# New durations and a shape-change term in the clock that orders a hybrid encoder kernel

## Chip, cores and metric

The kernel runs on one core of a Trainium2 chip. The metric is the time of one execution in microseconds of device time; the time before is the median of three runs.

## What is computed

One layer of a streaming encoder, for 512 prompt tokens and 8 x 16 sample tokens (640 rows, 1024 wide, all float32). Two mixers read one projection of the normalised input; their outputs are gated, merged and projected.

```python
h = rmsnorm(x); proj = h @ w_in                # q,k,v,z_A | g_A,g_B | r,k,v,lora_w,lora_a,z_B
# A: stick-breaking attention, 16 heads x 64, s < t only
z = q @ k.T / 8
later = reverse_cumsum(log_sigmoid(-z)) - log_sigmoid(-z)
o_a = exp(log_sigmoid(z) + later) @ v
# B: RWKV-7 recurrence, 16 heads, state S of 64 x 64
S = S * w_t + (S @ -kk_t) (kk_t * a_t) + v_t k_t ;  o_b = S @ r_t
y = sig(g_A) * ((o_a * silu(z_A)) @ w_o_a) + sig(g_B) * ((norm(o_b) * silu(z_B)) @ w_o_b)
out = rmsnorm(x + y @ w_out)
```

## The kernel before, in words

The kernel is one static program: a Python function emits every instruction in order, and each engine works through its own queue in that order, held only by semaphores.

Projections are jobs of 128 output columns (`gemm_range`): two halves of 320 or 322 tokens, 8 depth tiles, and three matmuls for each (weights and activations are split into a high and a low part, `whi`, `wlo` and `xh`, `xl`, in the fp32r type), all into the PSUM tile `ps_g`. They are the filler: after every 6 matmuls the generator yields. The split of the next job's weights (`wsplit` on ScalarE, `wlow` on VectorE) stands at fixed places in the job.

Everything else is a stream, a generator that yields the tiles its next step reads. For each of 8 head pairs of mixer B: `prep` (decay, keys, the tiles `H`, `BK`, `AB`), `prep2` (a triangular solve, 30 steps of two products on POOL in `INV` and `itmp`, then transposes through `STG`), `samp`, `chain` (8 recurrence steps of three PE parts: `X,H` into `RH`, `RH,AB` into `X`, `X,BKt` into the next `X`), `sstate` and `post`. For each of 8 head pairs of mixer A: `aprep` (loads, transposes) and `attn`, nine score items, each two sigmoids on ScalarE (`kp`, `bt`), a mask product on POOL, a reversed scan and a product on VectorE, four or fewer transposes by PE two items later (`flip`, into `wt`), and the product with the values (`pv`) one item after that.

What goes next is decided while the program is built, by `Driver.run` and `Clock`. Every engine call goes through `_Eng`, which computes a duration `d` by engine and operation and hands it to `Clock.note`; this keeps when each engine is free and when each tile is ready (end plus a hop `LAT` of 0.25 us, of which `near` is taken off on the same engine). The driver takes PE's clock as now. A stream whose tiles are ready by then steps at once, lowest priority number first; when none is, the projections emit 6 more matmuls. `SLACK` (3 us) holds the solver near PE, `CALM` (1.6 us) holds `prep` when VectorE's clock runs ahead, `MARGIN` (3 us) delays stores on SP's queue. All of these are in units of this clock. The clock is used only to build the order; it is no instruction.

The last six projection blocks (`w_o_a`, `w_out`) run after the streams, in a fixed order.

Of the kernel before, what the change touches and what calls it, by code (L numbers as in the profile page):

```python
# [26 lines left out]
F32 = mybir.dt.float32  # L27
F32R = mybir.dt.float32r
# [53 lines left out]
class Clock:  # L82
# [5 lines left out]
    def __init__(self):  # L88
        self.free = dict(pe=0.0, act=0.0, dve=0.0, pool=0.0, dma=0.0)
        self.ready = {}  # L90
        self.by = {}
        self.used = {}
        self.rings = {}
        self.closed = 0.0
        self.tbl = None
        self.last = {}
        self.near = dict(pe=0.25, act=0.2, dve=0.2, pool=0.15, dma=0.0)
        self.wire = 0.0

    def bank(self, tag, bufs, name):  # L100
# [46 lines left out]
def _name(ap):  # L147

    if not hasattr(ap, "tensor"):
        return ap  # L150
    n = ap.tensor.name
    return f"{n}:{ap.offset % (8 * T) // T}" if n in PARTS else n


def _cols(ap):
    n = 1
    for d in ap.shape[1:]:
        n *= d
    return n
# [30 lines left out]
class _Eng:  # L190
# [3 lines left out]
    def __getattr__(self, op):  # L194
        f = getattr(self.obj, op)

        def call(*a, **k):
            r = f(*a, **k)  # L198
            aps = [x for x in list(a) + list(k.values()) if hasattr(x, "tensor")]
            out = k.get("out", aps[0])  # L200
            ins = [x for x in aps if x is not out]
            n = _cols(out)
            e = self.eng
            lat = Clock.LAT
            if e == "pe":
                w = k.get("lhsT")
                if w is None:
                    d = 0.115
                else:
                    m = _cols(w)  # L210
                    if w.dtype == F32R:
                        d = max(n / 2360.0, 0.107)
                    elif w.dtype == F32:
                        d = max(0.026 + n * 0.00087, 0.082 if m > 32 else 0.041) if m <= 64 else 0.005 + n / 600.0
                    else:
                        d = 0.06
            elif e == "act":
                d = 0.05 + n * 0.00086 + 0.1 * sum(hasattr(k.get(x), "tensor") for x in ("scale", "bias"))
                fn = str(k.get("func"))
                t = "sig" if "Sigmoid" in fn or "Tanh" in fn else "exp" if "Exp" in fn else \  # L220
                    "sqrt" if "Sqrt" in fn else None
                if t is not None and t != self.clk.tbl:
                    self.clk.tbl = t
                    d += 1.28
            elif e == "dve":
                d = 0.066 + n * 0.00105
                if "scalar" in op:
                    d += 0.03 * sum(hasattr(x, "tensor") and _cols(x) == 1 for x in list(a) + list(k.values()))
                if op == "reciprocal":
                    d = 0.05 + n * 0.0064  # L230
            elif e == "pool":
                d = 0.15 + n * (0.0021 if op == "tensor_tensor" else 0.001)
                if op == "tensor_copy":
                    d = 0.2 + n * 0.0035
            else:
                d = 0.47
                run = 2.0 if min(x.shape[-1] for x in aps) < 128 else 1.0
                lat = (n * out.shape[0] * 4 * run / 3.6e5, 0.65, 0.93)
            self.clk.note(e, d, [_name(x) for x in ins], [_name(out)], lat)
            return r  # L240
        return call
# [1455 lines left out]
```

## Time and profile before

| what | value |
|---|---|
| median of three runs | 1240.88 us (1238.41 to 1241.9) |
| profiled execution | 1238.89 us, span 1237.1 us |
| PE busy, of the span | 1181.2 us, 95% |
| VectorE, ScalarE, POOL busy | 757.6, 616.6, 601.5 us |
| granted TensorE clock, mean | 0.979 |

All times of the trace are us from the span's start. The span is four stages: a start to 41 us; projections with mixer B's streams, the recurrence stage, to 745 and with its last streams to 835; projections with mixer A's streams, the attention stage, to 1085; then projections alone. A busy PE is one with some matmul under way; matmuls overlap, and a projection matmul lasts 0.31 us while the next starts 0.15 us after it. A granted clock of 1.00 is 2.4 GHz, 0.50 is 1.2 GHz; other values are means over both. One float32 matmul of the program with few columns can stand as two in the trace.

### The profile page before, as it was taken

What the parts mean: (1) busy time and instruction counts of PE and PEld (TensorE: products, weight loads), DVE (VectorE), ACT (ScalarE), POOL (GpSimd) and SP (SyncE); (2) the same over time, 40 slices, a digit from 0 to 9 for tenths busy, and PEclk for the clock granted to TensorE, in tenths of its full rate; (3) what the DMA queues carried; (4) which work ended last, traced back from release to release, by engine and by line L of the source; (5) the groups of instructions that cost most, each with busy time, mean ns of one, the idle gap of its engine ahead of it and who ended that gap; (6) DMA issues with size and microseconds to landing.
All of it is one profiled execution on the core that took longest, in us unless ns stands there. A gap on an engine that the chain in (4) does not pass through costs nothing.

```text
span 1237.1 us, 24609 instructions
## 1 busy us (share of the span) xinstructions
PE 1181.2 (95%) x9538; PEld 1033.0 (84%) x9538; DVE 757.6 (61%) x1460; ACT 616.6 (50%) x1307; POOL 601.5 (49%) x867
## 2 busy tenths in 40 slices
PE   7999989999999999999999999999999989999997
PEld 5989977888878988878888797897777757899997
DVE  5475674965765767857658443337667787655334
ACT  5624446555556664574565563535555444513223
POOL 1032947728539659477395671034444473313302
PEclk8989999999999999999999999999999988999999
DMA  6232312222313313223133243388665577255322
GB/s 183 73 105 60 95 51 51 85 88 50 113 46 89 91 41 89 79 63 95 46 80 106 55 125 92 97 214 214 159 151 137 140 190 175 61 182 186 95 86 86
DMA packets 205292, 130.65 MB, mean 106 GB/s; under 512 B 78332, under 2 KB 184696, under 8 KB 205176
## 3 DMA queue, kind: packets, MB, share of 16 engines
q1 hardware_dynamic: 204888, 129.03, 37.3%
q8 instruction: 75, 1.23, 0.4%
q14 instruction: 41, 0.34, 0.1%
q0 software_dynamic: 288, 0.05, 0.0%
HBM read 97.70 MB, written 31.35 MB: 104 GB/s over the span
## 4 chain that ended last, share of the span: by engine, by line
PE 70%; DVE 13%; POOL 6%; ACT 6%; issue 3%; DMA 2%; SPq 0%; DVEq 0%; ACTq 0%; POOLq 0%
PE ps_g L198 47%; PE ps_a L198 10%; PE ps_b L198 8%; PE ps_c L198 4%; DVE kp L198 2%; POOL itmp L198 2%; DVE bt L198 1%; POOL INV L198 1%; ACT STG L198 1%; DVE wlo L198 1%; DMA raw<-in_w_o_a_dram 1%; ACT AB L198 1%; DVE xl L198 1%; DVE BK L198 1%; DVE Oa L198 1%
## 5 line engine op out<-in xcount | busy, mean ns | idle before, releaser
L198 PE MATMUL ps_g<-xh,whi 128*128 128x320 f32 (+1 forms) x1424 | 479.0, 336 | 1.3 <-ACT xh L198 1.3
L198 PE MATMUL ps_g<-xl,whi 128*128 128x320 f32 (+1 forms) x1424 | 445.4, 313 | 4.1 <-DVE xl L198 4.1
L198 PE MATMUL ps_g<-xh,wlo 128*128 128x320 f32 (+1 forms) x1424 | 445.4, 313 | 4.0 <-DVE wlo L198 4.0
L198 PEld LDWEIGHTS ps_g<-xh,whi 128*128 128x128 f32 x1424 | 271.5, 191 | 25.6 <-issue 10.4
L198 PEld LDWEIGHTS ps_g<-xl,whi 128*128 128x128 f32 x1424 | 272.0, 191 | 6.1 <-DVE xl L198 5.3
L198 PEld LDWEIGHTS ps_g<-xh,wlo 128*128 128x128 f32 x1424 | 271.4, 191 | 4.8 <-DVE wlo L198 4.8
L198 POOL TENSOR_TENSOR itmp<-INV 128x30 f32<-128x30 f32 (+14 forms) x240 | 138.3, 576 | 80.0 <-DVE INV L198 64.9
L198 POOL TENSOR_TENSOR INV<-INV,itmp 128x30 f32<-128x30 f32 (+14 forms) x240 | 146.2, 609 | 18.8
L198 DVE TENSOR_TENSOR wlo<-raw,whi 128x1024 fp32r<-128x1024 f32 x97 | 126.0, 1299 | 42.6 <-ACT whi L198 41.6
L198 ACT ACTIVATE whi<-raw 128x1024 fp32r<-128x1024 f32 x97 | 102.5, 1056 | 61.0 <-DMA raw<-in_w_o_a_dram 29.8
L198 POOL TENSOR_TENSOR bt<-bt,amsk 128x128 f32<-128x128 f32 x64 | 45.6, 716 | 130.6 <-ACT bt L198 62.0
L198 DVE TENSOR_TENSOR_SCAN kp<-kp,amsk 128x256 f32<-128x256 f32 (+3 forms) x80 | 75.8, 955 | 41.3 <-ACT kp L198 41.2
L198 ACT ACTIVATE sp<-ps_g 128x320 f32<-128x320 f32 x80 | 34.9, 437 | 84.6 <-PE ps_g L198 64.2
L198 ACT ACTIVATE kp<-ps_a 128x512 f32<-128x512 f32 (+3 forms) x72 | 33.1, 459 | 79.2 <-PE ps_a L198 61.9
L198 DVE SCALAR_TENSOR_TENSOR X<-ps_b,wc,SW 64x64 f32<-64x64 f32 x96 | 27.1, 283 | 73.4 <-PE ps_b L198 69.7
L198 POOL TENSOR_TENSOR ux<-X,cst 128x256 f32<-128x256 f32 x32 | 22.1, 713 | 98.2 <-DVE X L198 72.9
L198 ACT ACTIVATE RH<-ps_b 128x64 f32<-128x64 f32 (+1 forms) x64 | 15.1, 237 | 106.2 <-PE ps_b L198 106.0
L198 ACT ACT_TABLE_LOAD x39 | 50.0, 1283 | 10.6 <-DVE BK L198 6.0
L198 POOL TENSOR_TENSOR on<-on,V 128x640 f32<-128x640 f32 x8 | 13.0, 1621 | 86.6 <-ACT on L198 86.6
L198 DVE TENSOR_TENSOR bt<-bt,kp 128x511 f32<-128x511 f32 (+4 forms) x72 | 43.8, 608 | 9.4 <-POOL bt L198 2.9
L198 PE MATMUL ps_a<-H,BK 64*128 64x128 f32 x320 | 48.1, 286 | 0.7 <-DVE H L198 0.4
L198 PE MATMUL ps_b<-cst,bt 128*128 128x128 f32 x192 | 36.0, 294 | 12.9 <-DVE bt L198 12.4
(244 smaller groups left out, 2289.8 us busy)
## 6 DMA issues: line engine op xcount, KB each, us to landing
raw<-in_w_in_dram SPq DMA_DIRECT2D x81, 512.0 KB
q<-dr_q SPq DMA_DIRECT2D x32, 160.0 KB
Kr<-in_cache_sb_k_dram SPq DMA_DIRECT2D x16, 256.0 KB
Vp<-in_cache_sb_v_dram SPq DMA_DIRECT2D x16, 256.0 KB
raw<-in_w_o_b_dram SPq DMA_DIRECT2D x8, 512.0 KB
raw<-in_w_o_a_dram SPq DMA_DIRECT2D x8, 512.0 KB
oraw<-in_w_out_dram SPq DMA_DIRECT2D x4, 1024.0 KB
dr_zB<-zm SPq DMA_DIRECT2D x8, 320.0 KB
```

The lines of the kernel that those rows point to most:

```text
L198: r = f(*a, **k)
```

## The change

It replaces the constants by which `_Eng` computes a duration, and adds a term for PE: the shape of the part of the array that a matmul uses (rows above 32 or 64, columns above 32 or 64, with everything above 64 x 64 as "full") is kept in `Clock.mode`; a matmul of another shape than the one before is charged 0.1 us more when the array was in full use, 0.2 otherwise. On ScalarE it charges operations on fewer than 128 and fewer than 64 partitions more; on VectorE it has own formulas for scan, scalar-tensor-tensor, tensor-scalar, bn_stats and the strided transpose, and 0.09 more for reading PSUM on fewer than 128 partitions; POOL's constants rise. The two `near` values shrink. `LAT`, `SLACK`, `CALM`, `MARGIN`, the DMA constants and the driver's rules stay. No instruction is added, removed or resized: what can change is the order in which they are emitted, and with it each engine's queue.

```diff
--- before.py
+++ after.py
@@ -94,7 +94,8 @@
         self.closed = 0.0
         self.tbl = None
         self.last = {}
-        self.near = dict(pe=0.25, act=0.2, dve=0.2, pool=0.15, dma=0.0)
+        self.near = dict(pe=0.25, act=0.15, dve=0.14, pool=0.15, dma=0.0)
+        self.mode = None
         self.wire = 0.0
 
     def bank(self, tag, bufs, name):
@@ -204,18 +205,26 @@
             lat = Clock.LAT
             if e == "pe":
                 w = k.get("lhsT")
+                m, r = (128, 128) if w is None else (_cols(w), w.shape[0])
                 if w is None:
-                    d = 0.115
+                    d = 0.109
+                elif w.dtype == F32R:
+                    d = max(0.013 + n / 2400.0, 0.107)
+                elif w.dtype == F32:
+                    d = max(0.026 + n * 0.00087, 0.082 if m > 32 else 0.041) if m <= 64 else \
+                        max(n / 600.0 + 0.005, 0.216)
                 else:
-                    m = _cols(w)
-                    if w.dtype == F32R:
-                        d = max(n / 2360.0, 0.107)
-                    elif w.dtype == F32:
-                        d = max(0.026 + n * 0.00087, 0.082 if m > 32 else 0.041) if m <= 64 else 0.005 + n / 600.0
-                    else:
-                        d = 0.06
+                    d = 0.089
+                mode = "full" if r > 64 and m > 64 else (r > 32, r > 64, m > 32, m > 64)
+                if mode != self.clk.mode:
+                    d += 0.1 if self.clk.mode == "full" else 0.2
+                    self.clk.mode = mode
             elif e == "act":
-                d = 0.05 + n * 0.00086 + 0.1 * sum(hasattr(k.get(x), "tensor") for x in ("scale", "bias"))
+                d = 0.065 + n * 0.00085 + 0.1 * sum(hasattr(k.get(x), "tensor") for x in ("scale", "bias"))
+                if out.shape[0] < 64:
+                    d = 0.12 + n * 0.0021
+                elif out.shape[0] < 128:
+                    d += 0.115
                 fn = str(k.get("func"))
                 t = "sig" if "Sigmoid" in fn or "Tanh" in fn else "exp" if "Exp" in fn else \
                     "sqrt" if "Sqrt" in fn else None
@@ -223,15 +232,26 @@
                     self.clk.tbl = t
                     d += 1.28
             elif e == "dve":
-                d = 0.066 + n * 0.00105
-                if "scalar" in op:
-                    d += 0.03 * sum(hasattr(x, "tensor") and _cols(x) == 1 for x in list(a) + list(k.values()))
-                if op == "reciprocal":
+                d = 0.075 + n * 0.00106
+                if op == "scalar_tensor_tensor":
+                    d = 0.13 + n * 0.00112
+                elif op == "tensor_scalar":
+                    d = 0.1 + n * 0.0011 + 0.03 * sum(hasattr(x, "tensor") and _cols(x) == 1
+                                                     for x in list(a) + list(k.values()))
+                elif op == "tensor_tensor_scan":
+                    d = 0.03 + n * 0.0025
+                elif op == "reciprocal":
                     d = 0.05 + n * 0.0064
+                elif op == "bn_stats":
+                    d = 0.126
+                elif op == "transpose" and len(ins[0].shape) > 2 and ins[0].ap[-1][0] > 1:
+                    d = 2.03
+                if out.shape[0] < 128 and any(_name(x).startswith("ps_") for x in ins if hasattr(x, "tensor")):
+                    d += 0.09
             elif e == "pool":
-                d = 0.15 + n * (0.0021 if op == "tensor_tensor" else 0.001)
+                d = 0.2 + n * (0.0022 if op == "tensor_tensor" else 0.0012)
                 if op == "tensor_copy":
-                    d = 0.2 + n * 0.0035
+                    d = 0.15 + n * 0.0035
             else:
                 d = 0.47
                 run = 2.0 if min(x.shape[-1] for x in aps) < 128 else 1.0
```

## Rows read from the trace of the kernel before

**Rows 1.** The page's sections 1 and 2: busy time of each engine, and PE's granted clock.
```profile
PE 1181.2 (95%) x9538; PEld 1033.0 (84%) x9538; DVE 757.6 (61%) x1460; ACT 616.6 (50%) x1307; POOL 601.5 (49%) x867
...
PEclk8989999999999999999999999999999988999999
```

**Rows 2.** Stretches: us, then busy us (x instructions), granted clock, DMA share, GB/s.
```profile
core 0: us, PE busy (x) PEld busy (x) DVE busy (x) ACT busy (x) POOL busy (x), PEclk, DMA share, GB/s
...
41.00:745.00 704.00, 683.57 (x5684) 596.98 (x5683) 458.06 (x959) 392.85 (x817) 427.80 (x660) 0.99 0.27 78
...
835.00:1085.00 250.00, 231.04 (x1876) 186.61 (x1875) 178.70 (x238) 121.19 (x286) 115.61 (x133) 0.95 0.61 152
1085.00:1209.00 124.00, 122.52 (x890) 121.99 (x889) 53.95 (x83) 31.34 (x52) 27.71 (x37) 1.00 0.43 137
```

**Rows 3.** PE's waits: what waited, for what, us in total, times, longest.
```profile
PE ps_b L198 <- DVE bt L198: 12.4, 15, 2.4
PE ps_g L198 <- DVE wlo L198: 4.7, 4, 2.1
PE ps_g L198 <- DVE xl L198: 4.1, 5, 2.2
...
PE ps_c L198 <- DVE sg L198: 2.9, 2, 1.6
...
PE ps_a L198 <- DVE STG L198: 2.5, 2, 1.9
```

**Rows 4.** Timeline, attention stage: start, us, engine, operation, [idle before <-releaser].
```profile
846.22 2.18 POOL L198 TENSOR_TENSOR sg<-sg,sz 128x640 f32<-128x640 f32 x1
...
847.17 1.64 DVE L198 TENSOR_TENSOR bt<-bt,kp 128x383 f32<-128x383 f32 x1
...
848.96 0.52 PE L198 MATMUL ps_b<-cst,bt 128*128 128x128 f32 x3 [1.81 <-DVE bt L198]
...
849.92 0.47 PE L198 MATMUL ps_g<-xh,whi 128*128 128x320 f32 x1
...
850.04 0.56 DVE L198 TENSOR_TENSOR bt<-bt,kp 128x383 f32<-128x383 f32 x1
...
850.18 0.47 PE L198 MATMUL ps_g<-xl,whi 128*128 128x320 f32 x1
```

**Rows 5.** The stretch that begins with the end of that wait (columns as in 2).
```profile
848.90:852.40 3.50, 3.44 (x24) 3.14 (x25) 3.26 (x6) 1.10 (x3) 2.62 (x4) 0.59 0.99 304
```

**Rows 6.** Timeline of PE, recurrence stage: one round with an RH step.
```profile
297.13 0.39 PE L198 MATMUL ps_g<-xh,whi 128*128 128x322 f32 x1
...
297.66 0.31 PE L198 MATMUL ps_g<-xh,whi 128*128 128x322 f32 x1
297.81 0.32 PE L198 MATMUL ps_g<-xl,whi 128*128 128x322 f32 x1
...
298.46 0.41 PE L198 MATMUL ps_g<-xh,whi 128*128 128x322 f32 x1
```

**Rows 7.** Stretches, instructions on tile ps_g alone (PE, PEld, DVE, ACT).
```profile
835.00:1085.00 250.00, 111.57 (x611) 92.35 (x610) 3.42 (x7) 8.04 (x18) 0.95 0.61 152
```

**Rows 8.** VectorE's groups by shape: xcount | busy us, mean ns | idle before.
```profile
L198 DVE TENSOR_TENSOR_SCAN kp<-kp,amsk 128x512 f32<-128x512 f32 x16 | 24.6, 1537 | 0.0
...
L198 DVE TENSOR_TENSOR_SCAN kp<-kp,amsk 128x384 f32<-128x384 f32 x16 | 18.7, 1172 | 0.0
```

**Rows 9.** ScalarE's groups by shape.
```profile
L198 ACT ACTIVATE X<-ps_b 64x64 f32<-64x64 f32 x128 | 27.9, 218 | 31.1 <-PE ps_b L198 29.0
...
L198 ACT ACTIVATE wt<-ps_b 128x512 f32<-128x512 f32 x24 | 14.4, 602 | 3.8 <-PE ps_b L198 3.6
...
L198 ACT ACTIVATE RH<-ps_b 128x64 f32<-128x64 f32 x56 | 12.5, 223 | 71.7 <-PE ps_b L198 71.5
```

**Rows 10.** The page's section 5: POOL's solver, all shapes together.
```profile
L198 POOL TENSOR_TENSOR itmp<-INV 128x30 f32<-128x30 f32 (+14 forms) x240 | 138.3, 576 | 80.0 <-DVE INV L198 64.9
L198 POOL TENSOR_TENSOR INV<-INV,itmp 128x30 f32<-128x30 f32 (+14 forms) x240 | 146.2, 609 | 18.8
```

## Prediction before the run

> **What bounds the kernel now.** I read the engine totals first: PE is busy 95% of the span, the other three between 49% and 61% [rows 1]. Then the stages. From 1085 to 1209 us only projection matmuls run, PE is busy 122.5 of 124 us and nothing the change touches is interleaved there; in the recurrence stage (41 to 745) PE is busy 683.6 of 704, in the attention stage (835 to 1085) 231.0 of 250 [rows 2]. So the time is a fixed sum of PE work plus three losses: PE waiting, PE at its lower clock, and the cost of stepping from projection matmuls into a stream's small ones and back. The change moves no instruction's work, only the order, so only these three can move.
>
> The waits [rows 3] name VectorE tiles above all: `bt`, the attention weights on their way to be transposed (12.4 us in 15 waits), and `sg` behind it (2.9); then `wlo` 4.7 and `xl` 4.1, which belong to the weight split and the reload, and `STG` 2.5. Of the 19 us that PE is idle in the attention stage, 15.3 are the first two. The lower clock is coupled to them: the granted clock is 0.95 in the attention stage against 0.99 and 1.00 in the others [rows 2], and one long wait shows why. At 848.96 PE has stood still 1.81 us, and the stretch that starts there is granted 0.59, mostly the 1.2 GHz level; projection matmuls then start 0.26 us apart (849.92, 850.18) [rows 4, 5], where at 2.4 GHz they start 0.15 apart [rows 6]. A deficit of 0.05 over 250 us is 25 us at the lower level; at 0.15 for 0.26 it costs 25 x 0.44, about 11 us. So some 26 us are at stake there, 15.3 of waiting and 11 of clock, and in the recurrence stage some 20 of waiting and (0.01 x 704 / 0.5) x 0.44 = 6 of clock.
>
> **The change, part by part.** The builder's clock decides how many projection matmuls go between a stream's steps: a step is emitted once the clock says that its input is ready. What counts is therefore not a constant by itself but its ratio to how fast PE's own clock runs.
>
> *PE's durations and the shape changes.* A round of six 322-wide projection matmuls and one `RH` step takes 1.33 us in the trace (297.13 to 298.46) [rows 6]. The old constants give 6 x 322/2360 + 2 x 0.082 = 0.98, the new ones 6 x 0.147 + 0.1 + 0.164 + 0.2 = 1.35. PE's clock is right now, and 1.37 times as fast in such a round. In pure projection it is 1.08 times as fast (0.1356 to 0.1463). In the attention stage 611 projection matmuls [rows 7] add 611 x 0.0107 = 6.5 us, and by the code each pair leaves the full array 15 times (2 past-key groups, 8 scores, 5 value steps): 8 x 15 x 0.3 = 36 us. That is 42.5 us on what was some 180 (231.0 busy less 11 of clock less 42.5): 1.23 times.
>
> *VectorE.* The scan is the gross error: 384 columns were 0.469 and become 0.990, 512 were 0.604 and become 1.310; the trace has 1.17 and 1.54 [rows 8]. Over the stage that adds 16 x 0.706 + 32 x 0.335 + 16 x 0.521 + 16 x 0.150 = 32.7 us to the clock's VectorE, whose busy time is 178.7 [rows 2], so that it grows 178.7 / 146 = 1.22 times if the rest was charged in full, and 149 / 116 = 1.28 times if the rest was a fifth short, as the product of 383 columns is (0.468 charged, 0.56 alone) [rows 4]. The path of one 384-wide item (sigmoid, scan, product, three hops of 0.25) goes from 2.07 to 2.61, 1.26 times. Against PE's 1.23 that leaves the single item 2% more PE work under it, and VectorE's queue, 22 us per pair, between nothing and 4% more: up to 1 us for each of the 8 pairs. I take a third of the 15.3 us, 5 us; bounds 0 and 15. The lower clock goes with the long waits: I take 4 of its 11, bounds 0 and 11.
>
> Where I stop short of more is one mechanism. In the wait at 848.96 the product of 383 columns took 1.64 us while POOL's 640-wide product ran (846.22, 2.18 us); the same product alone took 0.56 (850.04) [rows 4]. Neither set of constants has that. Four waits of 1.8 to 2.4 us, 8.0 of the 15.3, show this one pattern. The Trainium skill (Perfetto Trace Analysis, Optimizing Scalar/DVE Operations) states that GPSIMD and DVE share an SBUF read port which a two-port DVE operation holds exclusively; the trace agrees that they hinder each other, here with VectorE as the one that waits, 1.64 against 0.56. By that rule alone no duration for one operation repairs these four waits, and the sum would lose its first two terms.
>
> *ScalarE and half-height operations.* The copy of 64 partitions to `X` goes from 0.105 to 0.234 (trace 0.218), which with two of them and two hops makes 0.71 into 0.97, 1.37 times, as much as the round: the recurrence's chain keeps its one chunk per step. `RH` goes only from 0.105 to 0.119 (trace 0.223), the 512-wide `wt` from 0.49 to 0.50 (0.602) [rows 9]. Hops stay 0.25. Such plain edges lose real margin: `wt` with two hops had 0.99 x 1.23 = 1.22 us of PE work under it and gets 1.00; `RH` had 0.605 x 1.36 = 0.82 and gets 0.62. Both still cover the measured operation by about 0.4. The lower `near` values give back 0.05 where producer and consumer are on one engine. I add 4 us of new small waits; bounds 0 and 12.
>
> *POOL.* The solver was 2 x (30 x 0.15 + 4960 x 0.0021) = 29.8 us and becomes 33.8; the trace has (138.3 + 146.2) / 8 = 35.6 per pair [rows 10]. That is 1.13 times where PE's clock gains some 1.2, so PE would come 1.8 us earlier; the four 32-partition copies behind it (0.325 to 0.792 each) and the strided transpose (1.14 to 2.03) give 1.6 back. For `STG`, 2.5 us of wait [rows 3], I take 1 us of gain, bounds -4 and +3.
>
> *Queues.* SP's stores are flushed 3 us of PE clock after their data; with PE 1.2 times as fast that is at most 0.5 us earlier, and SP has other loads between. `wlo` and `xl` go by position in the projection, not by the clock: nothing, unless VectorE's queue shifts (bounds -4 and +4, inside the range). Shape changes are only counted, never avoided; since a step moves PE's clock further, a few more steps follow each other directly. The `RH` step costs 1.33 - 6 x 0.147 = 0.45 us, under half of it for the changes; with five to ten merged, -1, bounds -5 and +3.
>
> **Sum.** -5 - 4 + 4 - 1 - 1 = -7. The profiled execution took 1238.9 (span 1237.1); 1231.9 follows. The median of the three runs shown is 2.0 above that execution, so 1234.
>
> **The rivals.** *Cancelled* (1240): both sides of every comparison grow by the same 1.2 to 1.3, the order stays nearly as it was, the four long waits stay because of POOL. For it: the ratios above, 1.26 against 1.23. Against it: hundreds of decisions lie near their threshold, so some move. Between 1237 and 1244.6.
>
> *Thinner margins* (1252, slower): ScalarE's plain edges in the chain and the flips have some 0.2 us less PE work under them. It decides where the unmodelled part of ScalarE's queue exceeds the 0.4 that is left: a weight split `whi` or a table load just ahead does. If a third of the 64 `RH`, 64 `X` and 64 `wt` edges waited 0.2 us, that is 13 us, with the attention stage no better; 1238.9 + 13 - 2 (the `STG` and merging terms) + 2 (to the median) gives 1252. Against it: today ScalarE hardly stands among PE's waits.
>
> *Waits repaired* (1216): the scan was the whole cause. All of 15.3 and 10 of the 11 us of clock go, nothing new comes: 1238.9 - 25 + 2 = 1216. Against it stands POOL's product.
>
> **How the numbers follow.** Forecast (gain of 4 to 17 us) 0.42, cancelled 0.27, thinner margins 0.25, waits repaired 0.06. A difference of 0.3%, 3.7 us, is about what a measurement of this kernel can tell from none. Faster by more: 0.48; within: 0.27; slower: 0.25. The range from 1217 to 1254 leaves out most of the repaired case and the end of the slow one.
>
> **What would show it.** Right: `bt` and `sg` waits together near 10 us instead of 15.3, granted clock in the attention stage at 0.96 or 0.97, and PE's busy total hardly changed. Wrong: `bt` still above 12 with waits of 1.8 us and more (cancelled); or `RH`, `X` and `wt` from ScalarE among PE's first waits (thinner margins). If the total fell far more than waits and clock together, the cost of shape changes, which I hold nearly fixed, would be the step that failed.

## The result, and the profile after

The changed kernel takes 1278.36 us (1271.46 to 1281.22) where the kernel before takes 1240.2: a ratio of 1.030, 95% interval 1.025 to 1.0349. It is 38 us slower; forecast were 7 us faster, with a range that ended at 1254. The profiled execution is the quickest of the four, 1271.46 us with a span of 1269.7, so the traces have 32.6 us to explain (1269.7 - 1237.1).

The page's totals after, the rows that answer to [rows 1]:

```profile
PE 1198.4 (94%) x9538; PEld 1051.7 (83%) x9538; DVE 765.1 (60%) x1460; ACT 621.9 (49%) x1308; POOL 583.1 (46%) x867
...
PEclk9989999999989789799999999998999999988999
```

The matmuls are the same 9538, and PE is busy 17 us longer for them. The clock's row has dips to 8 and 7 in slices 12 to 17, in the middle of the recurrence stage, where before had nines throughout. The stretches of [rows 2], after:

```profile
41.00:745.00 704.00, 682.25 (x5511) 601.21 (x5510) 453.25 (x913) 375.24 (x775) 381.50 (x601) 0.95 0.26 75
835.00:1085.00 250.00, 231.46 (x1851) 194.42 (x1849) 163.08 (x245) 121.18 (x266) 98.52 (x120) 0.97 0.66 163
1085.00:1209.00 124.00, 109.42 (x772) 98.53 (x773) 68.87 (x103) 38.33 (x71) 44.97 (x60) 0.93 0.45 133
```

In the first 704 us PE is as busy as before (682.25 against 683.57) but gets 173 instructions fewer done, at a clock of 0.95 instead of 0.99. In the last stretch, which the prediction took as untouched, it is busy 109.4 us of 124 at 0.93, where it was 122.5 at 1.00. As everything has shifted, the stages have to be cut where they now begin. The attention stage runs from 835 to 1084 before and from 891 to 1127 after. Before:

```profile
41.00:835.00 794.00, 773.02 (x6430) 677.94 (x6430) 488.66 (x1036) 430.42 (x904) 443.52 (x675) 0.99 0.30 84
835.00:1084.00 249.00, 230.04 (x1870) 185.61 (x1869) 178.01 (x237) 121.19 (x286) 115.61 (x133) 0.95 0.61 153
1084.00:1237.00 153.00, 144.48 (x1068) 143.75 (x1068) 67.61 (x139) 40.62 (x78) 35.08 (x41) 0.98 0.39 128
```

And after:

```profile
41.00:891.00 850.00, 823.53 (x6644) 730.56 (x6643) 504.19 (x1038) 441.50 (x921) 432.58 (x675) 0.95 0.29 84
891.00:1127.00 236.00, 218.77 (x1828) 175.33 (x1826) 178.03 (x243) 119.34 (x273) 106.55 (x131) 0.99 0.61 148
1127.00:1270.00 143.00, 124.01 (x898) 121.02 (x896) 59.35 (x128) 36.46 (x74) 36.67 (x44) 0.93 0.38 125
```

The attention stage did what was forecast, and more: 236 us instead of 249, its clock 0.99 instead of 0.95. The recurrence stage takes 56 us more with 214 more instructions; the end has 170 instructions fewer and saves only 10 us.

**Where the 32.6 us come from.** I added up PE's gaps and the time that its clock's records stand at 0.50, stage by stage up to PE's last matmul. Of the latter I priced the part in which PE is busy at 0.44, the prediction's figure; the rest is among the gaps already. Recurrence: 5.5 us more idle, 78.5 us at the lower clock instead of 17.1 (busy in 77.3 of them instead of 16.8), which is 5.5 + 60.5 x 0.44 = +32.1. Attention: 17.2 idle instead of 19.0, 6.8 low instead of 23.9 (busy in 6.6 instead of 21.4), -8.3. After it: 11.5 idle instead of 1.5, 17.1 low instead of none (busy in 7.6), +13.3. Together +37; the remaining -4.5 fits PE's work itself: the order emitted has 840 changes of matmul shape instead of 876, counted in the traces, and at (0.45 - 0.164) / 2 = 0.14 for each, from the prediction's `RH` step, 36 of them are 5.

**The recurrence stage.** Stretches of after, columns as in [rows 2], all engines:

```profile
390.00:419.00 29.00, 29.00 (x225) 28.67 (x224) 24.52 (x44) 19.76 (x31) 22.38 (x33) 1.00 0.35 109
419.00:426.00 7.00, 6.55 (x94) 5.38 (x94) 6.78 (x11) 1.68 (x6) 1.79 (x2) 1.00 0.03 8
426.00:457.00 31.00, 31.00 (x161) 23.78 (x161) 12.52 (x29) 11.61 (x30) 3.41 (x5) 0.50 0.19 49
```

The same with the instructions on `ps_g` alone (PE, PEld, DVE, ACT, as in [rows 7]):

```profile
390.00:419.00 29.00, 27.87 (x186) 27.15 (x186) 2.19 (x7) 3.29 (x7) 1.00 0.35 109
419.00:426.00 7.00, 2.60 (x16) 2.07 (x16) 0.00 (x0) 0.44 (x1) 1.00 0.03 8
426.00:457.00 31.00, 8.85 (x30) 7.32 (x30) 0.00 (x0) 0.43 (x1) 0.50 0.19 49
```

From 426 to 457 PE is busy all 31.0 us, and its granted clock is 0.50, the 1.2 GHz level. What differs from the stretch ahead at full clock is what it is busy with: projection matmuls cover 8.85 of 31 us instead of 27.87 of 29. The timeline of PE (start, us), just ahead of that and in the middle of it:

```profile
422.65 1.16 PE L199 MATMUL ps_a<-H,BK 64*128 64x128 f32 x8
424.19 0.92 PE L199 MATMUL ps_b<-RH,AB 64*64 64x64 f32 x12 [0.39 <-DVE AB L199]
...
433.28 0.47 PE L199 MATMUL ps_g<-xh,wlo 128*128 128x320 f32 x1
433.68 0.48 PE L199 MATMUL ps_b<-X,H 128*64 128x64 f32 x4
...
434.31 2.07 PE L199 MATMUL ps_a<-H,BK 64*128 64x128 f32 x8
436.31 0.48 PE L199 MATMUL ps_b<-RH,AB 64*64 64x64 f32 x4
...
437.77 0.64 PE L199 MATMUL ps_a<-lat,wh 128*128 128x320 f32 x1
...
447.75 0.63 PE L199 MATMUL ps_g<-xh,whi 128*128 128x320 f32 x1
```

Between the projection matmuls at 433.28 and 447.75, 14 us, not one is emitted: the steps of the chain, the sample streams and the low-rank products follow one another, no wait among them. Every one costs about twice its time: `H,BK` 2.07 us where the same eight took 1.16 at 422.65.

How the clock falls has to be kept apart from how long it stays low. Ahead of the fall at 426 PE stood still 0.45 us in 7, and from 422.65 to 425.72 it had no projection matmul. But the second long stretch, 17.1 us from 525, came behind 2.96 us of waiting in 7 (518 to 525), and the other five falls of this stage behind 1.6 to 3.0. Before, the stage had four, each behind 1.5 to 2.2 us of waiting in 7, and each over after 3.4 or 6.8 us. What is new is less that the clock falls than that a busy PE stays at 1.2 GHz for 30.7 and 17.1 us.

**The end.** The six blocks after the streams need `oA`, reloaded and split. What used to lie between the end of the attention and that reload is the rest of the `w_o_b` projections, 30 us of them before (1084 to 1114). After, the attention ends at 1127 and they at 1132. The stretch of that reload, after:

```profile
1128.00:1153.00 25.00, 13.50 (x58) 10.88 (x57) 13.11 (x16) 5.69 (x6) 5.12 (x6) 0.66 0.68 224
```

Its two longest waits, in the timeline of PE:

```profile
1139.39 0.63 PE L199 MATMUL ps_g<-oAh,whi 128*128 128x320 f32 x1 [4.20 <-POOL oAh L199]
...
1148.38 0.64 PE L199 MATMUL ps_g<-oAl,whi 128*128 128x320 f32 x1 [5.03 <-DVE oAl L199]
```

PE's waits after, in answer to [rows 3]:

```profile
PE ps_b L199 <- DVE bt L199: 14.4, 26, 1.1
PE ps_g L199 <- DVE oAl L199: 7.1, 4, 5.0
PE ps_g L199 <- DVE wlo L199: 6.5, 5, 2.8
PE ps_b L199 <- DVE X L199: 6.1, 3, 3.0
...
PE ps_g L199 <- POOL oAh L199: 4.2, 1, 4.2
...
PE ps_g L199 <- DVE xl L199: 2.4, 4, 1.3
...
PE ps_b L199 <- ACT wt L199: 0.8, 2, 0.4
...
PE ps_b L199 <- ACT RH L199: 0.3, 1, 0.3
PE ps_a L199 <- DVE STG L199: 0.2, 1, 0.2
```

`bt` waits are more (26 for 15) and shorter (longest 1.1 for 2.4), `sg` is gone, `STG` nearly, and ScalarE's edges, the rival of thinner margins, take 1.1 us together. Before, `X`, `RH` and `wt` from ScalarE took 5.0, mostly in these two lines:

```profile
PE ps_a L198 <- ACT X L198: 2.5, 3, 1.5
...
PE ps_b L198 <- ACT RH L198: 1.8, 2, 1.2
```

### The profile page after: what moved, and what is told of

It reads as the page before. It is cut to its first block, busy times and chain, and to the rows that moved or that the text cites. A ratio compares the mean times of both kernels' runs of the same rounds, so it can differ in the third digit from the quotient of the medians.

```text
span 1269.7 us, 24608 instructions
## 1 busy us (share of the span) xinstructions
PE 1198.4 (94%) x9538; PEld 1051.7 (83%) x9538; DVE 765.1 (60%) x1460; ACT 621.9 (49%) x1308; POOL 583.1 (46%) x867
## 5 line engine op out<-in xcount | busy, mean ns | idle before, releaser
L199 PEld LDWEIGHTS ps_g<-xh,whi 128*128 128x128 f32 x1424 | 274.9, 193 | 25.7 <-issue 11.0
L199 PEld LDWEIGHTS ps_g<-xh,wlo 128*128 128x128 f32 x1424 | 274.4, 193 | 8.2 <-DVE wlo L199 8.2
L199 PEld LDWEIGHTS ps_g<-xl,whi 128*128 128x128 f32 x1424 | 275.2, 193 | 4.4 <-DVE xl L199 3.4
L199 POOL TENSOR_TENSOR itmp<-INV 128x30 f32<-128x30 f32 (+14 forms) x240 | 128.6, 536 | 134.8 <-DVE INV L199 118.4
L199 DVE TENSOR_TENSOR wlo<-raw,whi 128x1024 fp32r<-128x1024 f32 x97 | 125.7, 1296 | 44.4 <-ACT whi L199 43.7
L199 ACT ACTIVATE whi<-raw 128x1024 fp32r<-128x1024 f32 x97 | 102.4, 1056 | 52.8 <-DMA raw<-in_w_o_a_dram 28.2
L199 POOL TENSOR_TENSOR bt<-bt,amsk 128x128 f32<-128x128 f32 x64 | 44.6, 698 | 127.8 <-ACT bt L199 107.9
L199 DVE TENSOR_TENSOR_SCAN kp<-kp,amsk 128x256 f32<-128x256 f32 (+3 forms) x80 | 73.1, 922 | 32.6 <-ACT kp L199 32.4
L199 DVE TENSOR_TENSOR AB<-ps_a,cst 64x512 f32<-64x512 f32 (+1 forms) x48 | 28.7, 598 | 51.5 <-PE ps_a L199 51.2
L199 PE MATMUL ps_a<-H,BK 64*128 64x128 f32 x320 | 55.5, 317 | 2.3 <-DVE H L199 1.9
L199 PEld LDWEIGHTS ps_a<-H,BK 64*128 64x128 f32 x320 | 45.4, 213 | 10.2 <-issue 7.3
```

## The experiments

The theory after this reading: **the charge for shape changes merges the streams**. Each change of shape moves the builder's clock of PE by 0.1 or 0.2 us more, so that by the end of one stream's step another's tiles are ready; projections, which go only when no stream is ready, stay out, and PE does small matmuls alone, at 1.2 GHz. Its rivals: **thinner margins**, the new base durations bring PE to its tiles too early and it waits; and **a draw**, any other order costs or gains tens of us whatever the constants mean. The expectations call the first the bunching theory; their durations theory is that slower ScalarE, VectorE and POOL in the clock push the streams of successive head pairs together, and their systematic theory that the new constants cost time by what they say, on any order.

Each part was therefore run alone, most of them on a second order too, which a hop `LAT` of 0.255 instead of 0.25 gives. In the table below, each pair is us of PE's idle time / us at the lower clock, both up to PE's last matmul.

### The charge alone, and everything without it

The kernel before with the charge only:

```diff
+        self.mode = None
...
+                r = 128 if w is None else w.shape[0]
+                mode = "full" if w is None or (r > 64 and _cols(w) > 64) else (r > 32, r > 64, _cols(w) > 32, _cols(w) > 64)
+                if mode != self.clk.mode:
+                    d += 0.1 if self.clk.mode == "full" else 0.2
+                    self.clk.mode = mode
```

> The kernel before with the charge for a change of matmul shape (0.1 or 0.2 us) added and no other edit. Bunching theory: slower, 1260 to 1290, with 90 us or more at the lower clock and stretches of 20 us with hardly a projection. Durations theory: as before, 1236 to 1245. Thin-margin theory: PE runs faster against unchanged durations, so more waits, 1250 or more, but the lower clock only behind waits.

Measured: 1305.58 us, ratio 1.0526 (1.049 to 1.0562), worse than the whole change. Its longest stretch at the lower clock, all engines, then `ps_g` alone:

```profile
549.00:590.00 41.00, 40.89 (x202) 32.03 (x202) 18.78 (x39) 14.78 (x39) 6.49 (x10) 0.50 0.16 44
549.00:590.00 41.00, 15.38 (x49) 12.24 (x49) 0.00 (x0) 0.43 (x1) 0.50 0.16 44
```

PE's first waits:

```profile
PE ps_b L199 <- DVE bt L199: 22.1, 27, 2.2
PE ps_b L199 <- DVE X L199: 18.8, 8, 4.2
```

The same picture, longer: PE busy 40.89 of 41 us, projections 15.38 of it, 0.50. The fall itself came behind waiting: PE is busy 2.77 of the 7 us ahead (541.8 to 548.8). 112.6 us of the recurrence stage are at the lower clock instead of 17.1. It is not the clock alone: with the other engines' old, short durations against a quicker builder's clock of PE the waits grow too, 54.4 us idle instead of 21.0. A second order (`LAT` 0.255 in this kernel):

> A second draw of the charge alone: the kernel before with the charge for shape changes and with the hop at 0.255 us instead of 0.25. Bunching theory (the charge bunches the streams, whichever order it is): 80 us or more at the lower clock in the recurrence stage again, 1275 to 1310. Draw theory: anything between 1235 and 1300, and lower clock in the recurrence stage possibly as in the kernel before (17 us).

Two executions, 1297.43 and 1324.52, too far apart for a ratio; 102.4 us low and 52.0 idle in the recurrence stage. So the charge alone is slow on two orders, with the lower clock that was forecast.

The changed kernel without the charge:

```diff
                 if mode != self.clk.mode:
-                    d += 0.1 if self.clk.mode == "full" else 0.2
                     self.clk.mode = mode
```

> The changed kernel with all its new durations, but nothing charged for a change of matmul shape. Bunching theory (the charge moves PE's clock in the builder past the ready times of other streams, so that these step one behind the other without projections between, and PE falls to 1.2 GHz): time at the lower clock back from about 112 us to 40 to 60, 1235 to 1255 us. Durations theory (slower ScalarE, VectorE and POOL in the clock push the recurrences of successive pairs together): nothing changes, 1270 to 1285. Thin-margin theory: as durations, with the waits of PE no fewer.

Measured: 1277.01, ratio 1.0293 (1.027 to 1.0315). Taking the charge away brings nothing back, and as "the charge is all of it" my theory fell here; the time is the one that the durations theory forecast. The loss has moved in part. All engines, then `ps_g` alone:

```profile
824.00:851.00 27.00, 18.73 (x123) 13.88 (x124) 9.04 (x49) 14.04 (x39) 0.94 (x1) 0.50 0.10 23
...
1097.00:1136.00 39.00, 37.96 (x204) 25.37 (x198) 21.08 (x35) 17.25 (x43) 10.18 (x16) 0.50 0.11 27
...
824.00:851.00 27.00, 4.60 (x17) 4.72 (x18) 0.00 (x0) 0.00 (x0) 0.50 0.10 23
1097.00:1136.00 39.00, 0.04 (x1) 0.04 (x1) 0.00 (x0) 0.00 (x0) 0.50 0.11 27
```

The lower clock now stands above all at the two ends of the filler: the recurrence's projections are done at 817 with its streams running to 886, and those of `w_o_b` at 1089 with the attention running to 1136. (Another 23.9 us lie at 83 to 107, with PE busy and projections in 15 of them.) As I read it, with the other engines' durations raised and PE's steps hardly, the clock makes each stream wait longer and puts more projections between its steps, until there are none left; then the streams' small matmuls are alone, PE stands still 8.3 of the 27 us from 824, and the lower clock is back. That is a second way to the same loss: **the filler runs out**.

### PE's base durations, and the other engines'

The kernel before with PE's new durations, no charge (the branch of `e == "pe"` as in the change, without the line removed above):

> The kernel before with PE's new base durations (projections 0.146 instead of 0.136 us and so on), no charge for shape changes, everything else old. Bunching theory: little, 1235 to 1250. Durations theory: as before, 1236 to 1245. Thin-margin theory: PE 1.08 times as fast against the rest, some more waits, 1245 to 1255.

Measured: 1272.69, ratio 1.0248 (1.0218 to 1.0279). Its first waits:

```profile
PE ps_a L199 <- DVE STG L199: 12.2, 7, 2.5
PE ps_b L199 <- DVE bt L199: 10.2, 17, 1.8
```

On a second order (`LAT` 0.255):

> A second draw of PE's new base durations alone, without the charge, with the hop at 0.255 us. If PE's general rate against the rest bunches the streams: 60 us or more at the lower clock in the recurrence stage, 1265 to 1285. If only the charge does: 15 to 35 us there and 1235 to 1260.

1281.2, ratio 1.0326 (1.029 to 1.0362), `STG` 12.5 and `bt` 12.4. All three theories had put the first of these at 1255 or less, and the second has the time that mine forecast but 34.1 us low where it forecast 60. Here the margins are thinner: PE idles 71 and 81 us instead of 49. But the edges are VectorE's `STG`, behind POOL's solver, and not ScalarE's; in the whole change the other engines' new durations repair them (`STG` 0.2).

The kernel before with the new ScalarE, VectorE, POOL and `near` constants only:

> The kernel before with the new durations of VectorE, ScalarE and POOL and the new near values, PE's old. Bunching theory: no lower-clock stretches beyond those of before, 1230 to 1250. Durations theory: 1265 to 1285, streams late and the attention stage ending at 1115 or later. Thin-margin theory: the most PE work under every edge, so the fewest waits of all, bt below 8 us.

1269.14, ratio 1.0231 (1.0204 to 1.0258): the filler runs out again, and this too is what the durations theory forecast (1265 to 1285, the attention ending at 1115 or later: it ends at 1128). Its recurrence projections end at 795; from 800 to 844 the clock is at 0.50 and `ps_g` is busy 4.45 of 44 us. So no half of the change was good by itself; as I read it, each unbalances PE's clock against the rest. The durations theory does not cover the charge alone, which it had at 1236 to 1245.

### How far one order is a draw

Three of the old constants were moved by a hair, in the kernel before, each alone:

```diff
-                d = 0.066 + n * 0.00105
+                d = 0.067 + n * 0.00105
```

> The kernel before with one constant of the builder's clock moved by 1 ns: a VectorE operation is 0.067 + n x 0.00105 us instead of 0.066. As a description of the chip this is the same clock; the emitted order of PE first differs at 358 us of that clock, and a third of the positions hold another kind of matmul afterwards. Systematic theory (the new durations or the charge cost time by what they say): as before, 1236 to 1246 us. Draw theory (before is a favourable one of many orders that lie a nanosecond apart, and any edit of the clock draws anew): 1250 to 1285.

```diff
-                        d = max(n / 2360.0, 0.107)
+                        d = max(n / 2350.0, 0.107)
```

> The kernel before with a projection matmul of n columns charged n / 2350 us instead of n / 2360, 0.4% more; the order differs from 150 us of the clock on. Systematic theory: 1236 to 1246 us. Draw theory: 1250 to 1285.

```diff
-                d = 0.15 + n * (0.0021 if op == "tensor_tensor" else 0.001)
+                d = 0.151 + n * (0.0021 if op == "tensor_tensor" else 0.001)
```

> The kernel before with a POOL operation charged 0.151 + ... us instead of 0.15, 1 ns more; the order differs from 252 us of the clock on. Systematic theory: 1236 to 1246 us. Draw theory: 1250 to 1285.

Measured: 1233.93, ratio 0.9921 (0.988 to 0.9962), for 1 ns on VectorE; 1267.72, ratio 1.0184 (1.0071 to 1.0297), for 0.4% on a projection matmul; 1236.85, ratio 0.9967 (0.9933 to 1.0001), for 1 ns on POOL. So a change that means nothing moves this kernel by -7 to +27 us, and the draw is a real part of any single result here: the 1269 us of the other engines' durations hardly stands clear of 1267.7, the 1297 and more of the charge alone does. What it doesn't do is make the loss of the changed kernel: the recurrence stage of these four orders (with the kernel before) has 17 to 27 us at the lower clock. The slow one lost by waits (74 us idle) and by the end, where its attention finished after the `w_o_b` projections.

The changed kernel on a second order:

```diff
-    LAT = 0.25
+    LAT = 0.255
```

> The changed kernel with the hop between engines at 0.255 us instead of 0.25. Systematic theory: as the changed kernel, 1270 to 1282 us. Draw theory: another draw, 1245 to 1300, and the loss in other places (the stretch at the lower clock from 426 to 457 us gone).

1280.71, ratio 1.0289 (1.0171 to 1.0406). Again slow, and again by the lower clock: 109.2 us in the recurrence stage. One stretch (421 to 442) looks like the one above, PE busy 21.0 of 21 us and projections 8.47. Another does not; all engines, then `ps_g` alone:

```profile
159.00:183.00 24.00, 24.00 (x84) 20.54 (x83) 10.75 (x14) 7.44 (x13) 3.16 (x10) 0.51 0.27 78
159.00:183.00 24.00, 15.19 (x54) 13.51 (x53) 0.89 (x3) 1.48 (x3) 0.51 0.27 78
```

Here projections cover 15.19 of 24 us, so a PE left to small matmuls is not the whole account. The end is whole this time, 3.4 us low and 1.9 idle: of the two losses of the changed kernel the first comes back on another order, the second belongs to the order.

### Letting streams step earlier without any charge

To merge steps in the kernel before with its durations kept:

```diff
-                if at <= now + 0.02 and (best is None or s[:2] < best[:2]):
+                if at <= now + 0.3 and (best is None or s[:2] < best[:2]):
```

> The kernel before, every duration untouched, with a stream allowed to step when its tiles are ready within 0.3 us of now instead of 0.02. Streams bunch without any change of the clock's constants. Bunching theory: stretches of 10 us and more at the lower clock in the recurrence stage, 70 us or more in all, some more waits, 1260 to 1300. Durations theory: the lower clock stays behind waits alone; only waits grow, 1245 to 1265.

1268.13, ratio 1.0231 (1.0186 to 1.0276). The time is one that my theory forecast, but with 70 us or more at the lower clock in the recurrence stage; that goes from 17.1 to 41.0. Counted in the traces, the projections of that stage come in 166 separate groups here, against 250 before, 216 in the changed kernel, 184 with the charge alone and 255 in the changed kernel's second order. So this run has the most merged steps, and the order with 109.2 us low has no fewer groups than before: the number of merged steps alone does not account for the low time. What merging mostly bought here is waits (`bt` 15.9, `STG` 10.2, `X` 9.8), since steps that come early find their tiles not there.

### Keeping the streams apart, with the durations untouched

If merged steps are the loss, a rule that puts projections between them must take it away while the charge and all durations stay. The driver gets one: once the builder's clock of PE is 2.0 us past the end of the last projection step, projections go next if they can, although a stream is ready.

```diff
+    def may(self, gate, need, now):
+        return (gate is None or gate()) and self.clk.at(need) <= now + 0.02
...
-        gate, done, need = None, False, []
+        gate, done, need, since = None, False, [], 0.0
...
-            if best is not None:
+            if best is not None and (done or now - since < 2.0 or not self.may(gate, need, now)):
...
+                        since = self.clk.free["pe"]
```

> The changed kernel, clock and charge untouched, with one rule more in the driver: when PE's clock is 2.0 us past the last projection step, the projections go next even if a stream is ready. Bunching theory: the streams no longer run without projections, so the lower clock in the recurrence stage falls from 78 us to 30 or less, and the time to 1225 to 1245. Draw theory (the loss is that of an unlucky order, and a new order is a new draw): 1235 to 1285 with the lower clock anywhere between 20 and 110 us. Thin-margin theory: the waits stay, 1260 to 1275.

1241.86, ratio 1.0021 (0.9989 to 1.0054): 36 us back. With 1.5 instead of 2.0:

> The same with 1.5 us in place of 2.0, which is another order altogether. Bunching theory: as with 2.0, lower clock in the recurrence stage at 30 us or less and 1225 to 1245, so two orders agree. Draw theory: the two differ by tens of us.

1233.88, ratio 0.9945 (0.992 to 0.9971). With 1.2:

> A fourth order of the changed kernel with the rule, at 1.2 us. Bunching theory: 1228 to 1250, between the three others with the rule (1234, 1242, 1253), with the lower clock in the recurrence stage at 60 us or less. Draw theory (the rule's three orders were lucky against the changed kernel's two, 1278 and 1281): 1255 or more.

1226.69, ratio 0.9874 (0.984 to 0.9907), the quickest kernel here, ahead of both. Its timeline of PE in the chain of the recurrence stage:

```profile
399.75 1.16 PE L199 MATMUL ps_a<-H,BK 64*128 64x128 f32 x8
400.83 0.42 PE L199 MATMUL ps_g<-xh,whi 128*128 128x320 f32 x1
...
401.67 0.31 PE L199 MATMUL ps_g<-xh,wlo 128*128 128x320 f32 x1
401.91 0.34 PE L199 MATMUL ps_b<-X,H 128*64 128x64 f32 x4
...
402.29 0.42 PE L199 MATMUL ps_g<-xh,whi 128*128 128x320 f32 x1
```

Its stages:

```profile
41.00:835.00 794.00, 774.09 (x6375) 676.73 (x6376) 489.22 (x1034) 429.72 (x902) 439.82 (x675) 0.98 0.29 83
835.00:1085.00 250.00, 242.97 (x1991) 200.84 (x1990) 181.44 (x242) 125.30 (x292) 111.37 (x133) 0.98 0.64 160
```

And PE's wait for `bt`:

```profile
PE ps_b L199 <- DVE bt L199: 4.8, 11, 0.7
```

Six projections stand between two steps, `H,BK` takes 1.16 us, the 250 us from 835 hold 115 PE instructions more than before's (1991 against 1876), and `bt` costs 4.8 us instead of 12.4.

The rule on the kernel before (1.5):

> The kernel before with the same rule at 1.5 us of its own clock. Bunching theory: the lower clock in the recurrence stage stays at 17 to 25 us, so there is little to win: 1225 to 1250, the upper end if the streams, now slower, end after the projections that cover them. Draw theory: 1235 to 1285.

1253.24, ratio 1.0099 (1.008 to 1.0119). The rule is no gain in itself: there was little lower clock to win back (17.1 us low, now 34.1, where 17 to 25 were forecast), and this order ends its attention at 1110 with the `w_o_b` projections at 1114, so the end is bare again (17.1 low, 10.7 idle).

The rule (1.5) on the changed kernel's second order:

> A second draw of the changed kernel with the 1.5 us rule, with the hop at 0.255 us. Bunching theory: 30 us or less at the lower clock in the recurrence stage, 1228 to 1248. Draw theory: 1235 to 1285.

1252.92, ratio 1.0103 (1.0057 to 1.0148): 28 us less than that order without the rule, but 58.0 us of its recurrence stage are low, in three stretches of 14 to 17 us and two shorter; forecast were 30 us or less and at most 1248. The three begin behind 1.4 to 2.2 us of waiting in 7, as the falls of before do; why the level then lasts 14 to 17 us there, with projections in between, I did not settle.

The rule (1.5) without the charge:

> The new durations and the 1.5 us rule, without the charge. Bunching theory: the recurrence stage has little lower clock, but the clock now takes PE for faster than it is, so more projections go under every step, and the streams end after the projections that cover them: 1255 to 1285 with the loss behind 1090 us. If the charge is of no use once the rule is there: 1230 to 1245.

1266.82, ratio 1.0208 (1.0173 to 1.0243). Where the filler has run out no rule can put any: `ps_g` is busy 0.39 us between 1106 and 1125, at 0.50. On this order at least, then, the rule does not do without the charge.

| kernel | recurrence | attention | after it |
|---|---|---|---|
| before | 21.0 / 17.1 | 19.0 / 23.9 | 1.5 / 0.0 |
| changed | 26.5 / 78.5 | 17.2 / 6.8 | 11.5 / 17.1 |
| changed, second order | 30.1 / 109.2 | 17.1 / 13.7 | 1.9 / 3.4 |
| before + charge; second order | 54.4 / 112.6; 52.0 / 102.4 | 22.5 / 20.5; 23.3 / 13.7 | 0.9 / 0.0; 0.9 / 0.0 |
| changed, no charge | 27.6 / 64.9 | 8.8 / 52.4 | 10.8 / 22.7 |
| before + PE's durations; second order | 44.6 / 64.8; 50.3 / 34.1 | 15.7 / 13.7; 20.6 / 34.1 | 2.3 / 6.8; 1.4 / 0.0 |
| before + the other engines' | 30.1 / 54.6 | 15.3 / 41.0 | 10.5 / 17.1 |
| before, VectorE + 1 ns | 23.2 / 27.3 | 15.5 / 13.7 | 0.7 / 0.0 |
| before, projection + 0.4% | 38.3 / 23.9 | 18.1 / 13.7 | 9.8 / 17.1 |
| before, POOL + 1 ns | 24.3 / 17.1 | 16.2 / 13.7 | 1.1 / 0.0 |
| before, streams 0.3 early | 45.2 / 41.0 | 17.9 / 34.1 | 1.1 / 0.0 |
| changed + rule 2.0 | 27.5 / 27.3 | 8.6 / 20.5 | 1.8 / 0.0 |
| changed + rule 1.5 | 25.1 / 23.9 | 9.0 / 3.4 | 3.3 / 0.0 |
| changed + rule 1.2 | 19.9 / 34.1 | 7.0 / 10.2 | 0.7 / 0.0 |
| changed + rule 1.5, second order | 22.1 / 58.0 | 15.4 / 17.1 | 0.7 / 0.0 |
| before + rule 1.5 | 27.8 / 34.1 | 11.7 / 17.1 | 10.7 / 17.1 |
| changed, no charge, rule 1.5 | 28.3 / 44.4 | 8.9 / 43.4 | 9.9 / 21.5 |

## Why the prediction was wrong

**The step that failed** is the last one of the queues: "a few more steps follow each other directly", priced at -1 with bounds -5 and +3, as PE's own work. There its sign was right, though not its size: 36 changes of shape fewer, some 18 merged steps net where five to ten were supposed, and about -5 us. (By its own figures the -1 was small: of the 0.45 us of the `RH` step 0.29 are the changes, not "under half", so that five to ten merged steps are worth -1.4 to -2.9.) What was missing is the other side. The prediction tied the lower clock to waiting ("The lower clock is coupled to them") and so had no term for a PE that is busy without a gap and granted 1.2 GHz. Waits still begin most of the falls, but in the recurrence stage waiting grew by 5.5 us and the time at the lower level by 61.4, +27, which no bound of mine held. The text did name the place: the cost of shape changes as the step that failed "if the total fell far more"; the total rose instead. That the rule gives 36 us back at 2.0, 44 at 1.5 and 52 at 1.2 with every duration kept is the evidence that it is the placing of the steps and not the durations. In the recurrence stage it does so by the clock: idle time stays at 27.5, 25.1 and 19.9 us, from 26.5, and the low time falls from 78.5 to 27.3, 23.9 and 34.1, 20 to 24 us at 0.44; the rest is fewer waits in the attention stage and a whole end. What in the placing holds the clock down stays open in part: the longest stretches have few projections, but the run with the most merged steps has 41.0 us low, and several orders have stretches of 14 to 24 us with projections in more than half.

**The premise on the last stage.** "Nothing the change touches is interleaved there" held for the instructions and not for the cover: 30 us of `w_o_b` projections stood behind the attention only because of how many had gone between its steps. Under five us of them were left, and the reload of `oA` came bare, +13. As the second order doesn't have it, that term was one of range, not of sign; I had none.

**The attention stage** came out in kind and not in its parts. `bt` and `sg` together: 15.3 forecast to fall to 10, measured 14.4, nearly all of the -5 missing. The lower clock: -4 forecast, -6.5 measured (14.8 us of busy time x 0.44). They fit together through the length: waits of up to 2.4 us became 26 of at most 1.1, and the clock went from 0.95 to 0.99 with almost the same sum. So the coupling that I read from one wait [rows 4, 5] seems to be one to long waits; this is argued from two kernels, and of the two falls left, at 989 and 1057, the second has 0.54 us of waiting in the 7 us ahead. With the rule the waits go too: 6.9 and 4.8 us of `bt`, no `sg`.

**POOL's product.** The argument that four waits can't be repaired, since no duration knows that the 383-column product takes 1.64 us beside POOL, fell. Over 16 such products, three lasted 1.5 us and more before, five after and six with the rule of 1.2, up to 1.94, so the hindrance is still there. The Trainium skill (Perfetto Trace Analysis, Optimizing Scalar/DVE Operations) says that GPSIMD and DVE share an SBUF read port, and the trace agrees that they hinder each other: POOL's 640-wide product ran during 1.1 to 1.5 us of each of these. (The fourth of the prediction's waits, at 1043.74, is not this product but the scan ahead of it: 2.29 us at 1040.65 for a mean of 1.17 [rows 8], beside POOL's 2.51 us at 1039.61.) But the longest wait for `bt` is 1.1 and 0.7: with VectorE paced slower in the clock, more work of PE stands ahead of the transpose. That this work is what covers the product I argue; I did not follow each of the products.

**Small terms.** `STG` was forecast to lose 1 of its 2.5 us and lost 2.3. The +4 for ScalarE's plain edges came out as -4: their waits went from 5.0 us to 1.1 (`wt` 0.8, `RH` 0.3). `wlo` and `xl` moved from 8.8 to 8.9 together, as said. The step of PE's durations, 1.35 by the clock for 1.33 in the trace [rows 6], stands; a builder's clock that is nearer to the time emitted the order that runs 78.5 us of this stage at 1.2 GHz.

**The rivals.** "Thinner margins" had the right side and 1252, but not by its mechanism: ScalarE's edges hardly wait, and where margins do thin, with PE's durations alone, it is `STG` and `bt`. "Cancelled" and "waits repaired" are out. Missing was a rival in which the order makes PE slow instead of idle, and a view for it was there: `ps_g` fills 491.6 of the 704 us before, so how thickly the other matmuls could come to lie was a question to ask.

**What stays open.** Whether the new durations are worth anything. On four orders each, the old constants took 1240.2, 1233.9, 1236.9 and 1267.7, the new ones with the rule 1226.7, 1233.9, 1241.9 and 1252.9: means of 1244.7 and 1238.9, nearer to each other than the orders of either. Only the loss without the rule (1278.4 and 1280.7) stands clear of that, on two orders. The end of the filler was made worse and better by orders, but not repaired by itself; and neither the lower clock left in the rule's second order nor that of the changed kernel's second order at 159 to 183 has a cause shown.

## What to carry to other kernels

A planner that knows every duration can still make a worse order, if its clock doesn't know what the work does to the engine's speed: give it a rule for that (here, large matmuls among the small ones), and a view of how much filler is left for the work that needs cover. Read the granted clock beside the busy share, by stage, before and after, since a slow PE looks fully used. And before a change of a planner's constants is judged, run two or three orders that differ by nothing meaningful: here four of them spread over 34 us.

## What the runs showed of the hardware

PE stood at 1.2 GHz while it was busy almost without a gap: 31.0 of 31 us at 0.50 (426 to 457, after) with projections in 8.85 of them, 40.89 of 41 at 0.50 (549 to 590, charge alone) with 15.38, and 24.00 of 24 at 0.51 (159 to 183, the changed kernel's second order) with 15.19. In each the rest were float32 matmuls of the streams, many of them on part of the array. It was back at 2.4 GHz when projections filled most of PE again (457 to 520, after: granted 1.00, 63.0 of 63 us busy, 51.5 by projections). Ahead of the first of the three PE was busy 6.55 us of 7, ahead of the second 2.77, ahead of the third 5.00. The Trainium skill (TensorE: Matmul & The Clock Gate, HAM oscillation — how this bites in real kernels) tells of the lost clock as one of gaps in which PE is idle. That bears on how most of the falls here begin; while the three stretches last there is hardly any gap, and the measurement decides. The small matmuls pay for it as the large do: `H,BK` x8 takes 2.07 us at 0.50 and 1.16 at 1.00, a projection starts 0.26 us after the one before instead of 0.15.
